# Gated, scaled and summed weights of the merge and Fourier output, prepared in the input stage and kept in DRAM

## The chip, the core and the metric

The kernel runs on one core of a Trainium2 chip. Its time is the device time of one execution in microseconds (us); the median of three runs is given. A profiled execution has a span, from its first to its last instruction, which is slightly shorter than its time.

## What is computed

One transformer block over 2048 latent tokens of width 1024, with 256 context tokens. The parts that matter here:

```python
hx = modulate(rms_norm(x, norm1_g), sh1, sc1)
fx, qx, kx, vx = split_projection(hx @ w_in)
y_four = fourier_mix(fx)                        # 4 groups of 128 channels, 2-D Fourier transform
y_attn = neighbourhood_attention(qx, kx, vx, kc, vc, rpb)
g_f, g_a = split(sigmoid(hx @ w_gate))
merged = g_f * (y_four @ w_fo) + g_a * (y_attn @ w_ao)
x = x + g1 * (merged @ w_o)
x = x + g2 * sqrelu_mlp(modulate(rms_norm(x, norm2_g), sh2, sc2), w1, w2)
```

w_fo and w_ao are 512 x 1024, w_o is 1024 x 1024, g1 is a vector of 1024 that comes from the conditioning c.

## The kernel before

Every large product is done with operands that are split in two: a rounded high half and the rest as low half, and three products (high-high, high-low, low-high) are summed by `mm3` (line 77) into one PSUM bank. So each weight must be brought to two halves before it is used: `split_on` (line 85) rounds on ScalarE (ACT) and subtracts on VectorE (DVE) or GpSimd (POOL); `halve` (line 385) does the same with a power-of-two scale.

The stages, in order:

1. **Input stage.** `run_pair` (line 767) goes through eight pairs of weight blocks in the order of `seq` (line 689): f, two gate blocks, q0 with a gate block, q1 with a gate block, v, k0 with a gate block, k1 with a gate block, and a last pair of gate blocks. Within a pair it loops over four blocks of 512 tokens (and the context tokens for k and v). Beside the matmuls run generators: `side_work` (line 294) computes the modulation vectors (g1r, the gates g1 in all 128 rows, among them), then loads all MLP weights once in 32 loads of 1 MB (w12m) to find their scales: 16 with a DVE maximum, 16 with an ACT square whose sum is accumulated. `split_values` (line 838) prepares v. When side_work ends, `early_blocks` (line 373) prepares eight blocks of MLP weights (N_EARLY), each of 1 MB, as seven scaled halves with `prepare` (line 389), and stores them in DRAM. `tick` (line 457) sets their pace: after each small unit of matmuls (a tick) it takes one step of side_work, and once that has ended, a share of a step of early_blocks (0.6 in a q or k unit, 0.8 in v, 1.5 in a gate unit). What is left of both is run out before the last pair.
2. **Last pair and `fourier_prep` (line 866).** Beside the last pair, fourier_prep folds the Fourier input and splits the tables. In its loop it also loads w_attn_out, w_out and w_fourier_out in eight loads of 1 MB (wn) and squares them on ACT, for their norms.
3. **Fourier stage.** `channel_dft`, `seq_dft`, `seq_dft64`, and `merge_scales` (line 995), which computes from the norms and the largest Fourier value the powers of two that keep the halves in range (mgs), and divides g1r by one of them.
4. **Attention.** 64 tiles of 128 queries (`order`, line 1104), two heads each, by `block` (line 1286). All loads through `fetch` (line 1048) are tied into one order on the SP queue. Beside the blocks `step` (line 1413) takes steps of `beside_attention` (line 1397): first `merge_fourier` (line 1168), which loads the rows of w_fourier_out and their mirrored rows wfr (`load_w`, line 1183), adds and subtracts them, splits the four results (ws), splits the Fourier output (ys), and does the products pmf; then `load_wa` (line 1389), which loads w_attn_out in four parts and scales, rounds and subtracts on POOL; then, from tile (3, 0, 3) plus three, `attn_out(0)` (line 1359), the merge of the first 256 tokens (products pua).
5. **Merge.** `attn_out(1)` runs while `stage_wo` (line 1522) brings w_out in eight parts through two staging buffers: DVE multiplies by g1r, ACT rounds, POOL and DVE in turn subtract (line 1536). Then for each 256 tokens: `out_proj` (line 1458, products po), `attn_out` for later tokens, and `norm_T`. PSUM has four banks for pua and po together, and the gate tiles ga, gf, ft have two buffers each.
6. **MLP.** Its weights come in halves from DRAM; the blocks that were not prepared early are prepared beside its matmuls (`prep`, line 1699) at a pace worked out from their number (`todo`, line 1783).

Within one engine, and within the SP queue, instructions run in the order in which they were queued. That order is planned when the kernel is built, from the order of the program and estimated times.

## Time and profile before

| | us |
|---|---|
| median of three runs (2656.83 to 2659.85) | 2658.93 |
| the profiled execution, time | 2660.88 |
| the profiled execution, span | 2659.1 |
| TensorE (PE) busy | 2538.6 |
| VectorE (DVE) busy | 1827.3 |
| ScalarE (ACT) busy | 1183.3 |
| GpSimd (POOL) busy | 484.4 |

A busy time is a sum over all stages, and each stage has its own limit. So the stretches of the kernel are looked at one by one (in the table of stretches, below, each engine's busy time is followed by its instructions as x and a number; PEld is TensorE's weight load): an engine that is busy for nearly the whole of a stretch sets its length, and idle time of another costs nothing there.

### The profile page before, as it was taken

The numbers are of one execution on the slowest core, as the hardware profiler recorded it, in microseconds if no ns is written. First come the engines' busy times: TensorE is split into PE (matmuls) and PEld (weight loads), VectorE is DVE, ScalarE is ACT, GpSimd is POOL, SyncE is SP. The second block draws the span as 40 slices with busy tenths as digits, with TensorE's granted clock in tenths as the row PEclk, the third lists the DMA queues.
The fourth block names the chain that finished last, engine by engine and source line by source line (L and its number), as shares of the span: only waits on it lengthen the run. The fifth ranks groups of instructions, "written<-read, shape, count | busy, mean of one in ns | idle before, by whom it ended". The sixth has DMA issues, their size and how long they took to land.

```text
span 2659.1 us, 42665 instructions
## 1 busy us (share of the span) xinstructions
PE 2538.6 (95%) x15830; PEld 1473.0 (55%) x15830; DVE 1827.3 (69%) x3672; ACT 1183.3 (44%) x2113; POOL 484.4 (18%) x715
## 2 busy tenths in 40 slices
PE   6899989898999899998999999999999999999999
PEld 5445756776656678875666444444444444444444
DVE  6756976568553678887777696978877644636367
ACT  5623225545242577874444564627351333314050
POOL 1201221012224545452000121121211100000000
PEclk9999999999999999998999999999999999999999
DMA  8577689867374744556767777787766533333334
GB/s 269 137 225 204 203 248 304 270 204 245 93 249 141 199 118 138 148 169 207 237 226 264 260 242 261 231 279 233 268 235 230 181 99 105 101 103 99 104 103 155
DMA packets 345962, 517.77 MB, mean 195 GB/s; under 512 B 48497, under 2 KB 210505, under 8 KB 341401
## 3 DMA queue, kind: packets, MB, share of 16 engines
q1 hardware_dynamic: 296425, 406.50, 48.8%
q0 software_dynamic: 29104, 75.23, 8.4%
q10 hardware_dynamic: 20224, 33.31, 3.9%
q8 instruction: 124, 2.03, 0.3%
q14 instruction: 85, 0.70, 0.1%
HBM read 370.11 MB, written 145.84 MB: 194 GB/s over the span
## 4 chain that ended last, share of the span: by engine, by line
PE 68%; DMA 11%; DVE 11%; issue 3%; ACT 3%; POOL 3%; SPq 2%; DVEq 0%; ACTq 0%; POOLq 0%
PE p L82 21%; PE pm L82 17%; PE ps_g L82 8%; PE po L82 6%; DMA w12m<-in_w_mlp 3%; PE pua L82 2%; PE ps_k L82 2%; PE tp L1325 2%; PE pmf L1263 2%; PE pv L1339 1%; SPq L188 1%; PE ps_f L82 1%; PE ps_v L82 1%; PE sc L1303 1%; DVE wo L387 1%
## 5 line engine op out<-in xcount | busy, mean ns | idle before, releaser
L82 PE MATMUL pm<-hc,wb 128*128 128x512 f16 x2688 | 582.6, 379 | 5.6 <-DVE p L1605 2.1
L82 PE MATMUL p<-wb,a 128*128 128x512 f16 x2688 | 581.9, 379 | 2.1 <-DVE X L1605 1.5
L82 PEld LDWEIGHTS <-wb 128*128 128x128 f16 x2688 | 262.9, 98 | 323.6 <-issue 7.3
L82 PEld LDWEIGHTS <-a 128*128 128x128 f16 x2688 | 263.0, 98 | 319.7 <-issue 2.9
L82 PE MATMUL ps_g<-hx,w_g 128*128 128x512 f16 x1536 | 342.5, 380 | 0.9 <-ACT ot_f L516 0.9
L1605 DVE TENSOR_TENSOR X<-X,p 128x512 f32<-128x512 f32 x280 | 184.5, 685 | 171.1 <-PE p L82 151.8
L82 PEld LDWEIGHTS <-hx 128*128 128x128 f16 x2304 | 227.4, 99 | 39.6 <-issue 7.2
L82 PEld LDWEIGHTS <-w_g 128*128 128x128 f16 x1536 | 151.0, 99 | 171.2 <-issue 3.2
L1091 POOL DMA_DIRECT2D bt<-tT x264 | 132.4, 508 | 76.3 <-DVE ri L1332 53.0
L1605 DVE TENSOR_TENSOR u<-pm,u 128x512 f32<-128x512 f32 x128 | 87.5, 690 | 84.3 <-PE pm L82 82.5
L1312 DVE CUSTOM_DVE_ANT_0 s<-sc,bt,qsc 128x736 f32<-128x736 f32 (+5 forms) x128 | 111.2, 869 | 37.1 <-PE sc L1306 33.9
L386 ACT ACTIVATE wo<-ws,msc 128x512 f16<-128x512 f32 x96 | 69.0, 718 | 152.0 <-DVE ws L430 124.0
L1609 ACT ACTIVATE p<-pm 128x512 f32<-128x512 f32 x32 | 18.9, 589 | 239.7 <-PE pm L82 239.7
L1739 POOL DMA_DIRECT2D xr<-x1d x32 | 17.3, 539 | 569.8 <-DVE X L1605 562.1
L1333 DVE SCALAR_TENSOR_TENSOR pL<-tp,pH 128x640 f16<-128x640 f32 (+1 forms) x128 | 112.3, 878 | 5.0 <-ACT pH L1328 4.5
L1316 ACT ACTIVATE s<-s,m 128x736 f32<-128x736 f32 (+5 forms) x128 | 104.6, 817 | 16.5 <-DVE m L1312 13.9
L386 ACT ACTIVATE wo<-raw,msc 128x512 f16<-128x512 f32 x128 | 87.4, 709 | 52.0 <-DVE raw L430 17.8
L82 PE MATMUL po<-wouH,mH 128*128 128x512 f16 x256 | 97.3, 384 | 9.3 <-DVE ga L1383 9.3
L1325 PE MATMUL tp<-ident,s 128*128 128x128 f32 x704 | 103.1, 281 | 0.8 <-ACT s L1316 0.7
L516 ACT ACTIVATE ot_g<-ps_g,usc_g 128x512 f32<-128x512 f32 x64 | 43.4, 681 | 130.9 <-PE ps_g L82 117.6
L82 PE MATMUL po<-wouL,mH 128*128 128x512 f16 x256 | 98.8, 386 | 2.4 <-POOL wouL L1536 2.4
L387 DVE SCALAR_TENSOR_TENSOR wo<-raw,msc,wo 128x512 f16<-128x512 f32 x128 | 94.4, 748 | 8.0 <-ACT wo L386 7.9
(535 smaller groups left out, 4645.9 us busy)
## 6 DMA issues: line engine op xcount, KB each, us to landing
wb<-w1d SPq DMA_DIRECT2D x224, 256.0 KB
wb<-w2d SPq DMA_DIRECT2D x224, 256.0 KB
w12m<-in_w_mlp SPq DMA_DIRECT2D x32, 1024.0 KB
raw<-in_w_mlp ACTq DMA_DIRECT2D x24, 1024.0 KB
w1d<-wo POOLq DMA_DIRECT2D x84, 256.0 KB, 4.0
w2d<-wo POOLq DMA_DIRECT2D x84, 256.0 KB, 4.0
gT<-ot_g SPq DMA_DIRECT2D x64, 256.0 KB
hc<-hcd SPq DMA_DIRECT2D x14, 1024.0 KB
```

The source lines that it names most:

```text
L82: last_mm[0] = pe.matmul(ps, l, r, start=(start and i == 0), stop=(stop and i == n - 1))
L188: last_load[0] = sp.dma_start(dst, src)
L386: act.activation(hi, src, AF.Copy, scale=scale)
L387: dve.scalar_tensor_tensor(out=lo, in0=src, scalar=scale, in1=hi, op0=ALU.mult, op1=ALU.subtract)
L516: act.activation(o, ps, func, scale=scale)
L1091: load_(t[i * 16:(i + 1) * 16, :, off + j0 * w:off + (j0 + 8) * w], raw(tT[ct], (2 * hp * 15 + dr) * w, [[120 * w, 16], [15 * w, 2], [1, 8 ...
L1263: pe.matmul(ps, l, r, start=(i == 0), stop=(i == len(prods) - 1))
L1312: tail["dve"] = dve.tensor_tensor_reduce(out=s[:, :n], in0=sc, in1=bias, op0=ALU.add, op1=ALU.min, scale=qsc[:, 4:5], scalar=3.0e38, accum ...
L1316: tail["act"] = act.activation(s[:, :n], s[:, :n], AF.Exp, bias=m1[:, 0:1], scale=-1.0, accum_out=m1[:, 1:2])
L1325: tail["pe"] = pe.transpose(tp[:, i * 128:(i + 1) * 128], s[:, o:o + 128], ident)
L1333: tail["dve"] = dve.scalar_tensor_tensor(out=pL[:, :c], in0=tp[:, :c], scalar=PTOP, in1=pH[:, :c], op0=ALU.mult, op1=ALU.subtract)
L1605: last["dve"] = dve.tensor_tensor(out=o, in0=x, in1=y, op=op)
```

## The change

The halves of w_attn_out (waD), of w_out times g1r (woD), and of the sums and differences of the mirrored rows of w_fourier_out (wfD) are made earlier and stored in DRAM. The eight wn loads and their squares move from fourier_prep into side_work, two to a yield, and the part of merge_scales that needs only the norms and g1r moves behind them (`branch_scales`). waD and woD are made in `branch_weights`, at the end of early_blocks. N_EARLY goes from 8 to 7, and the share of a step per q or k unit from 0.6 to 0.85. wfD is made at the end of fourier_prep. merge_fourier, load_wa and the merge then load ready halves.

```diff
@@ dit_block, side_work: after the loop over w12m
+        for j in range(8):
+            w, k = branch_rows(j)
+            wt = pb.tile([128, KT, 256], F32, tag="awt", name=f"wn{j}", bufs=2).rearrange("p k n -> p (k n)")
+            sp.dma_start(wt.rearrange("p (k n) -> p k n", k=2), w[k * 256:(k + 1) * 256, :].rearrange("(k p) n -> p k n", p=128))
+            act.activation(wt, wt, AF.Square, accum_out=wn[:, j:j + 1])
+            if j % 2:
+                yield
+        branch_scales()
...
+    def branch_scales():
+        ps = adp.tile([128, 512], F32, tag="ad", name="pwn")
+        pe.matmul(ps[:, 0:8], ones, wn, start=True, stop=True)
...
+        dve.reciprocal(mgs[:, 0:1], mgs[:, 10:11])
+        dve.reciprocal(y, mgs[:, 11:12])
+        dve.tensor_scalar(out=g1r, in0=g1r, scalar1=y, scalar2=None, op0=ALU.mult)
+
+    def branch_weights():
+        for j in range(6):
+            w, k = branch_rows(j)
+            t = pb.tile([128, KT, 256], F32, tag="awt", name=f"wb{j}", bufs=2)
...
+            sp.dma_start(t, w[k * 256:(k + 1) * 256, :].rearrange("(k p) n -> p k n", p=128))
+            yield
+            for i in range(2):
+                o = pb.tile([128, D], F32, tag="xh", name=f"wbo{j}_{i}", bufs=5).bitcast(F16).rearrange("p (o n) -> p o n", o=2)
+                if j < 2:
+                    halve(o[:, 0], o[:, 1], t[:, i], mgs[:, 0:1])
+                else:
+                    dve.tensor_tensor(out=t[:, i], in0=t[:, i], in1=g1r, op=ALU.mult)
+                    act.activation(o[:, 0], t[:, i], AF.Copy)
+                    dve.tensor_tensor(out=o[:, 1], in0=t[:, i], in1=o[:, 0], op=ALU.subtract)
+                sp.dma_start((waD, woD)[j >= 2][k][:, i * 2 * D:(i + 1) * 2 * D], o.rearrange("p o n -> p (o n)"))
+                yield
...
-    prepared, N_EARLY = set(), 8
+        yield from branch_weights()
+    prepared, N_EARLY = set(), 7
...
@@ unit_qk
-            tick(0.6)
+            tick(0.85)
...
@@ fourier_prep
-            for j in (2 * i, 2 * i + 1):
...
-                sp.dma_start(tn, w[k * 256:(k + 1) * 256, :].rearrange("(k p) n -> p k n", p=128))
-                tn = tn.rearrange("p k n -> p (k n)")
-                act.activation(tn, tn, AF.Square, accum_out=wn[:, j:j + 1])
+        fold(1)
+        yield
+        for p in range(2):
...
+                sp.dma_start(w[o:o + 64], a["w_fourier_out"][0][r0:r0 + 64, :])
+                pool.memset(wm[o:o + 1, :D], 0.0)
+                sp.dma_start(wm[o + 1:o + 64, :D], wfr[2 * p + h])
+            dve.tensor_tensor(out=t, in0=w, in1=wm[:, :D], op=ALU.add)
+            dve.tensor_tensor(out=w, in0=w, in1=wm[:, :D], op=ALU.subtract)
+            yield
+            for x, src in enumerate((t, w)):
...
+                split_on(dve, o[:, 0], o[:, 1], src)
+                for i in range(2):
+                    sp.dma_start(wfD[x, i, p], o[:, i].bitcast(F32))
                 yield
-        fold(1)
...
@@ merge_fourier
-        rows = load_w(0, fetch)
         for p in range(2):
             for x in range(2):
                 fetch(ys[x][1][:, p].bitcast(F32), yF[p][x])
+        for x in range(2):
+            for i in range(2):
+                fetch(ws[x][i].bitcast(F32), wfD[x, i].rearrange("a p n -> p a n"))
         yield
         for p in range(2):
-            w, wm, t = rows
-            dve.tensor_tensor(out=t, in0=w, in1=wm, op=ALU.add)
-            dve.tensor_tensor(out=w, in0=w, in1=wm, op=ALU.subtract)
-            yield
-            split_on(dve, ws[0][0][:, p], ws[0][1][:, p], t)
-            if p == 0:
-                rows = load_w(1, pool.dma_start)
-            yield
-            split_on(dve, ws[1][0][:, p], ws[1][1][:, p], w)
-            yield
...
@@ beside_attention
-        wa = [pm.tile([128, 4, D], F16, tag="wa" + o, name="wa" + o) for o in "HL"]
-        load_wa()
+        wa = pm.tile([128, 2, 2, 2, D], F16, tag="wa", name="wa")
+        for k in range(2):
+            fetch(wa[:, k].rearrange("p k o n -> p (k o n)"), waD[k])
...
@@ merge
     attn = attn_out(1, mmp, pg)
-    for k in range(8):
+    for k in range(4):
         next(attn)
-        wt = stage_wo(k)
-        dve.tensor_tensor(out=wt, in0=wt, in1=g1r, op=ALU.mult)
-        act.activation(wo[0][:, k, :], wt, AF.Copy)
-        (pool, dve)[k % 2].tensor_tensor(out=wo[1][:, k, :], in0=wt, in1=wo[0][:, k, :], op=ALU.subtract)
+        sp.dma_start(wo[:, k].rearrange("p k o n -> p (k o n)"), woD[k])
```

## Rows read from the trace of the kernel before

**Rows 1.** Page, part 1: busy us, share of the span, instructions.

```profile
PE 2538.6 (95%) x15830; PEld 1473.0 (55%) x15830; DVE 1827.3 (69%) x3672; ACT 1183.3 (44%) x2113; POOL 484.4 (18%) x715
```

**Rows 2.** Stretches: us, busy PE PEld DVE ACT POOL, clock, DMA share, GB/s.

```profile
240.00:340.00 100.00, 100.00 (x705) 70.24 (x703) 91.24 (x299) 34.18 (x76) 23.47 (x21) 1.00 0.76 220
374.00:455.00 81.00, 69.70 (x472) 46.68 (x473) 60.40 (x155) 36.09 (x67) 14.25 (x13) 0.96 0.92 300
455.00:500.00 45.00, 37.37 (x319) 31.54 (x317) 12.05 (x43) 23.73 (x39) 1.11 (x2) 0.96 0.79 261
600.00:640.00 40.00, 31.65 (x240) 23.22 (x238) 31.65 (x79) 17.50 (x37) 9.67 (x8) 0.98 0.85 270
660.00:760.00 100.00, 100.00 (x701) 68.96 (x700) 56.95 (x173) 34.30 (x66) 22.04 (x22) 1.00 0.41 125
760.00:840.00 80.00, 80.00 (x387) 38.14 (x385) 24.84 (x37) 31.28 (x47) 19.95 (x16) 1.00 0.64 220
889.80:912.00 22.20, 14.64 (x150) 11.24 (x150) 18.86 (x57) 15.54 (x31) 14.55 (x25) 0.92 0.86 229
890.00:942.00 52.00, 35.05 (x419) 27.51 (x417) 48.42 (x110) 40.35 (x80) 24.66 (x43) 0.93 0.67 166
1180.00:1214.30 34.30, 29.55 (x365) 25.51 (x364) 28.97 (x67) 22.48 (x52) 7.50 (x5) 0.95 0.46 141
1225.00:1234.00 9.00, 0.18 (x2) 0.11 (x2) 8.90 (x12) 2.53 (x3) 1.22 (x1) 0.71 0.91 320
1249.00:1261.30 12.30, 12.22 (x49) 5.19 (x49) 3.44 (x5) 2.21 (x3) 2.64 (x3) 0.86 0.73 235
1580.00:2000.00 420.00, 418.49 (x1939) 189.60 (x1938) 344.76 (x540) 209.33 (x337) 81.67 (x151) 1.00 0.76 253
```

**Rows 3.** On w_out's tiles: ns min/median/max, first and last start.

```profile
L1534 DVE TENSOR_TENSOR wou<-wou,g1r x8: 1212/1217/1224, 1192.4 to 1242.4; 128x1024 f32<-128x1024 f32 x8
L1535 ACT ACTIVATE wouH<-wou x8: 1041/1057/1058, 1220.7 to 1243.6; 128x1024 f16<-128x1024 f32 x8
L1536 POOL TENSOR_TENSOR wouL<-wou,wouH x4: 2115/2217/9937, 1221.8 to 1249.0; 128x1024 f16<-128x1024 f32 x4
```

**Rows 4.** PE's waits, whole span: us in total, times, longest.

```profile
PE po L82 <- DVE ga L1383: 9.3, 2, 8.8
PE ps_v L82 <- ACT vo_v L646: 6.5, 4, 3.7
PE po L82 <- POOL wouL L1536: 2.4, 1, 2.4
PE pua L82 <- POOL yaL L1366: 1.9, 1, 1.9
PE sc L1303 <- DMA Q<-qH: 1.9, 1, 1.9
```

**Rows 5.** Chain that ended last, PE pieces: start us, us, what.

```profile
512.79 2.63 PE ps_v L82 x24
1314.83 13.17 PE po L82 x61
1328.00 10.48 PE pua L82 x96
```

**Rows 6.** DVE groups, 890 to 942: count, busy us, mean ns, idle.

```profile
L1207 DVE TENSOR_TENSOR ws<-wf,wm 128x1024 f32<-128x1024 f32 x2 | 2.4, 1218 | 0.0
```

**Rows 7.** Timeline: last Q load of row block 1, its first matmul.

```profile
904.58 2.92 SPq L1051 DMA_DIRECT2D Ql<-qL  x2
912.00 0.31 PE L1303 MATMUL sc<-k,Q 128*128 128x360 f16 x1 [0.90 <-DVE m L1312]
```

**Rows 8.** Timeline: two ACT squares; and the early MLP blocks' halves on DVE.

```profile
455.97 1.91 ACT L340 ACTIVATE w12m<-w12m 128x2048 f32<-128x2048 f32 x1
486.83 1.91 ACT L340 ACTIVATE w12m<-w12m 128x2048 f32<-128x2048 f32 x1 [1.24 <-DMA w12m<-in_w_mlp]
L387 DVE SCALAR_TENSOR_TENSOR wo<-raw,msc,wo x32: 742/746/752, 499.3 to 669.6; 128x512 f16<-128x512 f32 x32
```

More of the change, by code (lines that the diff above doesn't have):

```diff
@@ L113, in dit_block @@
     wfr = scratch("wfr", [4, 63, D])
+    waD = scratch("waD", [2, 128, 4 * D], F16)
+    woD = scratch("woD", [4, 128, 4 * D], F16)
+    wfD = scratch("wfD", [2, 2, 2, 128, D])
     mF = scratch("mF", [8, 128, S])
@@ L1006, in merge_scales @@
         pe.matmul(ps[:, 0:1], ones[0:1, :], mgs[0:1, 6:7], start=True, stop=True)
-        pe.matmul(ps[:, 8:16], ones, wn, start=True, stop=True)
         dve.tensor_copy(y, ps[:, 0:1])
         ws = mgs[:, 7:10]
-        for i, (j, n) in enumerate(((0, 2), (2, 4), (6, 2))):
-            dve.tensor_reduce(out=ws[:, i:i + 1], in_=ps[:, 8 + j:8 + j + n], axis=AX.X, op=ALU.add)
-        pool.tensor_tensor(ws, ws, half[:, 0:3], op=ALU.pow)
         dve.scalar_tensor_tensor(out=b, in0=ws[:, 0:1], scalar=PTOP * VTOP * 512 ** 0.5, in1=vsc[:, 2:3], op0=ALU.mult, op1=ALU.mult)
@@ L1181, in merge_fourier @@
         ys = [pairs("ya"), pairs("yb")]
-        def load_w(p, fetch):
-            w, wm, t = (stage(f"w{o}{p}") for o in "fms")
-            for h in range(2):
-                o, r0 = 64 * h, (2 * p + h) * 128
-                fetch(w[o:o + 64], wf[r0:r0 + 64, :])
-                pool.memset(wm[o:o + 1], 0.0)
-                fetch(wm[o + 1:o + 64], wfr[2 * p + h])
-            return w, wm, t
         s64 = []
@@ L1203, in merge_fourier @@
                 fetch(ys[x][1][:, p].bitcast(F32), yF[p][x])
+        for x in range(2):
+            for i in range(2):
+                fetch(ws[x][i].bitcast(F32), wfD[x, i].rearrange("a p n -> p a n"))
         yield
         for p in range(2):
-            w, wm, t = rows
-            dve.tensor_tensor(out=t, in0=w, in1=wm, op=ALU.add)
-            dve.tensor_tensor(out=w, in0=w, in1=wm, op=ALU.subtract)
-            yield
-            split_on(dve, ws[0][0][:, p], ws[0][1][:, p], t)
-            if p == 0:
-                rows = load_w(1, pool.dma_start)
-            yield
-            split_on(dve, ws[1][0][:, p], ws[1][1][:, p], w)
-            yield
             for x in range(2):
@@ L1379, in attn_out @@
             for k in range(4):
-                mm3(ps, [(wa[0][:, k, ms], wa[1][:, k, ms], yH[:, k, :], yL[:, k, :])], k == 0, k == 3)
+                w = wa[:, k // 2, k % 2]
+                mm3(ps, [(w[:, 0, ms], w[:, 1, ms], yH[:, k, :], yL[:, k, :])], k == 0, k == 3)
                 if k == 1 and t == 0:
@@ L1387, in attn_out @@
             yield
-    def load_wa():
-        for k in range(4):
-            wt = pm.tile([128, D], F32, tag="wst", name=f"wao{k}", bufs=2)
-            fetch(wt, a["w_attn_out"][0, k * 128:(k + 1) * 128, :])
-            pool.tensor_scalar(wt, wt, mgs[:, 0:1], None, op0=ALU.mult)
-            pool.tensor_copy(wa[0][:, k, :], wt)
-            pool.tensor_tensor(wa[1][:, k, :], wt, wa[0][:, k, :], op=ALU.subtract)
     def beside_attention():
@@ L1448, in dit_block @@
     pg = sbuf("mgb", "right")
-    wo = [pg.tile([128, 8, D], F16, tag="wo" + o, name="wou" + o) for o in "HL"]
+    wo = pg.tile([128, 4, 2, 2, D], F16, tag="wo", name="wou")
     normed, x1s, x1r = {}, [], iter(range(0, S, 128))
@@ L1467, in out_proj @@
             ps = mmp.tile([128, 512], F32, tag="mm", name=f"po{nm}_{n}")
-            mm3(ps, [(mH[:, k, cs], mL[:, k, cs], wo[0][:, k, ns], wo[1][:, k, ns]) for k in range(KT)])
+            mm3(ps, [(mH[:, k, cs], mL[:, k, cs], *(wo[:, k // 2, k % 2, o, ns] for o in range(2))) for k in range(KT)])
             dve.scalar_tensor_tensor(out=x1[:, ns], in0=ps, scalar=mgs[:, 3:4], in1=x1[:, ns], op0=ALU.mult, op1=ALU.add)
```

36 lines of the change are left out of this document (19 added, 17 removed).

## The prediction, made before the changed kernel was run

> **What bounds the kernel now.** I read the busy totals first, then a table of stretches, then TensorE's (PE's) waits, and last single lines. PE is busy for 95% of the span [rows 1], so only what PE loses can be won, and what the added work makes it lose must be paid. The table of stretches [rows 2] shows where it loses. From 240 to 340, 660 to 760 and 760 to 840 us PE is busy the whole time: work beside it is free there. In 455 to 500 it loses 45 - 37.37 = 7.6 us, in 600 to 640 it loses 8.35. In 890 to 942, where attention starts, it is busy for 35.05 of 52 while VectorE (DVE) is busy for 48.42: DVE is the bound. From 1214.3 to 1261.3 (the entry to the merge) PE does 96 pua and 96 po matmuls; it is idle for nearly the whole of 1225 to 1234 and runs at a mean granted clock of 0.86 in 1249 to 1261.3. In the MLP (1580 to 2000) it loses 1.5 of 420. The profiled execution has a span of 2659.1 and a time of 2660.9; the median of the runs is 2658.9, 0.07% under it. The sum below is made on the profile and taken off the median.
>
> **What the change removes.**
> *Entry to the merge.* Eight loads of 512 KB through two staging buffers, eight DVE multiplications by g1r (1.217 each), eight ScalarE (ACT) roundings (1.057) and eight subtractions, four on DVE and four on GpSimd (POOL), the longest of these 9.94 us [rows 3]. PE waits 8.8 us for DVE and 2.4 for that POOL subtraction [rows 4]. At full speed 61 po matmuls take 13.17 us and 96 pua 10.48 [rows 5], 0.216 and 0.109 each, so 47 us hold 96 x 0.216 + 96 x 0.109 = 31.2 us of work: 15.8 are lost, of which 11.2 are waits and the rest is slow clock after them. DVE loses 8 x 1.22 + 4 x 1.22 = 14.6 us of work. What comes late next is data: the same 4 MB (now ready-made) cannot start before attention lets go of its buffers at about 1214, and 1225 to 1234 already moves 320 GB/s [rows 2]. 4.2e6 bytes at 320 are 13.1 us, so the last part lands at about 1227.5 and the gate tiles that queue behind it some 2 us later. PE stops at about 1225, so some 4.6 us of idling and 2 us of slow clock stay: gain 9. Bounds: 2.4 (only the POOL wait goes) to 15.8.
> *End of attention.* The POOL work of load_wa and its four 512 KB loads with their waits go; two 1 MB loads take their place. PE's 1.9 us for Q, queued behind those loads, and 1.9 for yaL go [rows 4], with some of the 34.3 - 29.55 = 4.75 us lost in 1180 to 1214.3 [rows 2]. I take 5; bounds 0 and 6.7.
> *Start of attention.* DVE loses eight passes of 1.218 us [rows 6] (two additions, two subtractions, four low halves) and two over the same 1,024 columns for g1r, in all ten, 12 us of the 48.42 [rows 2]. ACT loses four roundings. Against it stands a queue. SP loads 1 MB of rows and 2 MB of yF ahead of the Q of the next row block; now it loads 2 MB and 4 MB. That is 3 MB more, and at the 229 GB/s of 889.8 to 912 [rows 2] that takes 13.7 us. The last Q load was issued at 904.6 to 907.5 and its first matmul ran at 912.0 [rows 7], after a DVE wait: Q was in time by 4 us at most. So Q becomes late by some 10 us, while DVE uses the gap for the four splits of yF (four passes of the same length) that it now does after 912. 12 minus 10 plus part of those 4.9 leaves 3. Bounds: -9 (the splits don't move up) to +12 (Q lands in time).
> *Last pair and merge_scales.* Eight ACT squares (1.91 us for one of this shape [rows 8]) and their 8 MB leave the last pair; DVE gets 8 x 1.22 us, and 6 MB are loaded or stored. DVE is busy for 24.84 of 80 us there, PE for 80.00: nothing either way. If the tail slid past 840, it would delay the Fourier stage by up to 5.
>
> **What it adds.**
> *The v pair.* The eight 1 MB loads with their squares now run in side_work, two to a yield, after the 32 loads of the MLP weights. Eight of the 16 squares of w2 run from 455.97 to 486.83, 4.41 us apart, in a stretch where PE loses 7.6 us [rows 2, 8], since behind a square that waits for its load stand ACT's vo evictions, which free PSUM (6.5 us of PE's waits are on them [rows 4]) and whose stores queue on SP with the loads. That is 0.95 us of PE per load: eight more cost 7.6, take 8. Lower bound 0: from 240 to 340 loads at 220 GB/s cost PE nothing. Upper bound: if PE goes no faster than the squares, 8 x 4.41 = 35.3 us pass while the four ticks hold 4 x 2.63 = 10.5 us of PE work [rows 5]: 24.8. I take the near row, the same pair and queue. The matmul on wn and the chain of branch_scales wait for the last square; they are in the 8.
> *The k pairs.* branch_weights puts on DVE eight multiplications and eight subtractions of 1.22 and four low halves of about as much, 24.5 us; on ACT 12 x 1.06 = 12.7; and 12 MB on SP. One MLP block leaves (seven halves of 0.746 [rows 8] and four sums of about that on DVE, 8 us). Side_work ends four ticks later, and with 0.85 for 0.6 per tick the 68 steps just fit before the last pair. Its cover is 660 to 760, where DVE is idle for 43 us, ACT for 66, and the DMA share is 0.41. Cost 1; bounds 0 and 8, what 600 to 640 loses with a like mix.
> *The MLP.* One more block to prepare, 8 us of DVE beside 75 idle ones in 1580 to 2000: 1; bounds 0 and 2.
>
> Sum: -9 - 5 - 3 + 8 + 1 + 1 = -7, so 2658.9 - 7 = **2652**.
>
> **The rivals.**
> *The added loads are hidden* (chance 0.22). If the squares are queued where the loads have landed, the v pair costs 0 and the rest 2: -17 + 2 = -15, 2644. For it: 240 to 340. Against: the 7.6 us beside the same kind of load.
> *The merge is bound by its transfers* (0.15). po starts no earlier, since the gate tiles land behind 4 MB; only the POOL wait goes (2.4), attention's start gives nothing, its end 5: -7.4 + 10 = +2.6, 2661.5. For it: the DMA share of 0.91 in 1225 to 1234. Against: DVE busy for 8.90 of those 9 us.
> *Q waits for the weights* (0.10). Attention stalls at row block 1 by more than DVE gains, -9 in place of +3: -9 - 5 + 9 + 10 = +5, 2664. It decides if the Q loads land after about 920. The Trainium skill, "DMA: Bandwidth & Descriptors", section "Issuing engines are not separate DMA queues", speaks for this side: transfers from all issuing engines share the same 16 DMA engines, so the smaller load on the POOL queue would buy the SP queue no separate path. By the 358 GB/s of "SBUF — State Buffer", section "Summary: rules for kernel authors", the 3 MB would take an estimated 8.8 us and the start of attention would give about 7 in place of 3; no stretch above shows that rate.
> *The v pair runs at the pace of the loads* (0.17), the case on the slower side: -17 + 24.8 + 2 = +9.8, 2668.7. Its place is ACT's queue from about 487 us; it decides where two loads hold a tick for more than about 6 us. For it: 300 GB/s at a DMA share of 0.92 in 374 to 455, so twice the loads per tick can't all flow. Against: the v pair has 36 ticks, and nothing but queue order ties four of them to these loads.
>
> **The numbers.** My forecast has 0.36, from 2645 to 2658. About 0.2%, 5.3 us, is what a measurement of this kernel can tell from no change: faster means below 2653.6, slower above 2664.2. Faster: 0.27 of the forecast and all of the first rival, 0.49. Slower: most of the v pair's 0.17, half of the Q case and a little of the transfers, 0.22. The rest, 0.29, is no change. The range reaches from 2637 (loads hidden, merge and attention near their upper bounds) to 2669 (the v pair at its worst).
>
> **What would show it.** PE's 8.8 and 2.4 us before po, and its 1.9 us for Q and yaL: gone or cut to about 4.6 in all at the merge. In 890 to 942: DVE less full, and a PE wait on a Q load near 912 of at most 10 us. In the v pair: ps_v waits on vo of about 14 us in place of 6.5; over 25 would be the slower rival, none the hidden one. 660 to 840 should stay at full PE. The prediction is wrong as to mechanism if the time between 500 and 760 grows by more than 8 us, or if the merge keeps an idle stretch of 8 us with DVE no longer full.

## The result: slower by 0.4%, and the profile after

The changed kernel takes 2673.32 us (median of 6 runs, 2670.23 to 2677.69), the kernel before 2662.89 beside it (six runs, the three of the median 2658.93 among them): the ratio is 1.0041, with a 95% interval of 1.0026 to 1.0055. The forecast was 2652, with a range up to 2669 and a chance of 0.22 for slower. The profiled execution has a span of 2674.1 us, against 2659.1 before, so 15.0 us are to be found. The medians lie 10.4 apart, so some 4.6 of the 15.0 belong to these two executions and not to the change.

The work falls into stages whose bounds are the first and the last matmul on a tile (ps_v for the v pair, ps_k for the k pairs, pc for the Fourier stage, sc and pv for attention, po for the merge). First the changed kernel, by stretches with those bounds: v pair, k pairs, last pair, Fourier stage, attention, attention's end to the first po, merge, MLP. The columns are those of [rows 2].

```profile
448.50:565.60 117.10, 102.56 (x882) 88.11 (x881) 48.00 (x130) 71.75 (x107) 3.11 (x5) 0.96 0.84 280
565.60:767.50 201.90, 187.84 (x1302) 130.07 (x1300) 153.60 (x386) 87.51 (x159) 46.12 (x39) 0.97 0.70 232
767.50:856.30 88.80, 88.80 (x417) 40.83 (x416) 41.21 (x60) 24.78 (x41) 22.88 (x19) 1.00 0.56 193
856.30:909.40 53.10, 50.61 (x266) 41.30 (x265) 26.70 (x69) 11.17 (x31) 36.80 (x59) 0.87 0.67 179
909.40:1231.30 321.90, 300.51 (x3723) 248.02 (x3723) 263.89 (x591) 252.00 (x566) 131.25 (x255) 0.97 0.54 160
1231.30:1253.80 22.50, 10.65 (x100) 9.43 (x97) 8.30 (x17) 3.52 (x7) 0.00 (x0) 0.81 0.76 279
1253.80:1497.60 243.80, 243.66 (x1457) 144.60 (x1457) 165.81 (x331) 99.20 (x176) 10.16 (x15) 0.99 0.66 228
1497.60:2674.10 1176.50, 1163.70 (x5392) 527.51 (x5390) 803.97 (x1257) 451.77 (x728) 124.98 (x231) 1.00 0.57 186
```

The same stages of the kernel before:

```profile
448.80:556.10 107.30, 98.79 (x880) 86.47 (x879) 53.14 (x127) 60.98 (x96) 3.18 (x5) 0.98 0.82 272
556.10:748.20 192.10, 183.43 (x1302) 128.91 (x1300) 133.02 (x364) 76.04 (x146) 41.29 (x38) 0.98 0.53 169
748.20:837.00 88.80, 88.80 (x417) 40.87 (x416) 29.54 (x52) 35.71 (x53) 18.19 (x15) 1.00 0.65 215
837.00:889.90 52.90, 50.53 (x266) 41.49 (x265) 26.75 (x69) 11.17 (x31) 36.86 (x59) 0.87 0.63 171
889.90:1214.50 324.60, 299.99 (x3725) 246.79 (x3725) 275.30 (x613) 256.30 (x570) 162.18 (x276) 0.98 0.53 150
1214.50:1233.90 19.40, 10.58 (x98) 9.25 (x96) 16.39 (x22) 6.47 (x10) 4.39 (x2) 0.87 0.80 275
1233.90:1482.20 248.30, 245.49 (x1457) 145.05 (x1458) 174.20 (x338) 104.63 (x181) 22.18 (x17) 0.98 0.68 233
1482.20:2659.10 1176.90, 1163.79 (x5393) 527.51 (x5390) 797.25 (x1246) 448.09 (x721) 121.21 (x224) 1.00 0.56 183
```

The first column after the bounds is the length. The v pair is longer by 9.8 us and the k pairs by 9.8; the last pair, with PE busy in all of it, the Fourier stage and the MLP stand within 0.4. Attention gains 2.7, the way to the first po loses 3.1, the merge itself gains 4.5. So the input stage pays 19.6 and everything behind it gives back 4.1.

**Attention** hides two movements. Its first 96 score matmuls (three row blocks of the first heads) take 65.5 us in place of 72.4, so the start gives 6.9; from there to the end it takes 256.5 in place of 252.2, which loses 4.3. The stretch from the first score on, after and before:

```profile
909.40:931.00 21.60, 14.43 (x150) 10.88 (x150) 16.71 (x42) 16.41 (x33) 9.93 (x18) 0.92 0.90 308
...
909.40:961.40 52.00, 42.84 (x481) 32.76 (x481) 40.04 (x92) 40.30 (x86) 20.82 (x41) 0.93 0.64 199
```

```profile
889.90:911.50 21.60, 14.54 (x150) 11.20 (x150) 18.36 (x54) 15.09 (x30) 14.06 (x24) 0.92 0.86 226
...
889.90:941.90 52.00, 35.05 (x419) 27.49 (x419) 48.32 (x109) 40.35 (x80) 24.66 (x43) 0.94 0.67 166
```

DVE falls from 48.32 to 40.04 of 52 us and PE rises from 35.05 to 42.84. The first 21.6 us, with the 3 MB more, cost PE nothing (14.43 after, 14.54 before): they moved at 308 GB/s, where 226 had been reached before. At the end of attention the waits of PE, after and before:

```profile
PE pua L82 <- ACT yaH L1401: 2.2, 1, 2.2
PE pua L82 <- POOL yaL L1402: 2.0, 1, 2.0
PE pv L1375 <- DMA vt<-v: 1.7, 1, 1.7
PE sc L1339 <- DMA Ql<-qL: 1.5, 1, 1.5
...
PE sc L1339 <- DMA Q<-qH: 0.7, 1, 0.7
```

```profile
PE pua L82 <- POOL yaL L1366: 1.9, 1, 1.9
PE sc L1303 <- DMA Q<-qH: 1.9, 1, 1.9
PE pua L82 <- ACT yaH L1365: 0.8, 1, 0.8
```

The wait for yaL is still there, so it was not the work of load_wa: in the kernel before GpSimd had stood idle for 7.2 us ahead of that subtraction of 2.1 us; now a product (ft) that waited for its load stands just ahead of it. The waits for loads are 3.9 in place of 1.9: two loads of 1 MB stand ahead of Q and vt as four of 512 KB did. The size of this loss is uncertain: where the queues have the same order up to there, the stretch behind the first 96 score matmuls takes 252.4 to 256.8 us (after, e2, e5, e6 and e9 in the table below). The gain that was forecast is in none of them.

**The entry to the merge.** PE's wait for the gate (ga) grew from 8.8 [rows 4] to 11.8 us, and the wait for the GpSimd subtraction is gone (it came behind the first po, so its 2.4 us are part of what the merge gains). PE's waits from 1225 to 1262:

```profile
PE po L82 <- DVE ga L1420: 11.8, 1, 11.8
```

What SP's queue waited for from 1200 to 1260 (L1411 are the gate tiles, L1555 the weights), and the issues on its timeline:

```profile
SPq L1411 <- DVE ga L1421: 24.0, 6, 13.9
...
SPq L1555 <- DMA yA<-yo: 1.2, 1, 1.2
```

```profile
1220.27 0.92 SPq L1411 DMA_DIRECT2D gf<-gT  x1
1235.14 0.36 SPq L1411 DMA_DIRECT2D ft<-mF  x1
1237.14 1.99 SPq L1555 DMA_DIRECT2D wou<-woD  x4
1239.23 0.38 SPq L1411 DMA_DIRECT2D ft<-mF  x1
1239.66 0.50 SPq L1411 DMA_DIRECT2D ga<-gT  x1
```

SP issues nothing between 1221.2 and 1235.14, where a gate tile waits for its buffer (13.9 us); the weight loads come behind it, wait 1.2 us more for attention's last store (yA), start at 1237.14, and the gate tiles of the next rows (ft, ga at 1239) stand behind their 4 MB. The stretch that these take:

```profile
1237.10:1252.40 15.30, 4.83 (x45) 4.18 (x43) 3.76 (x8) 1.47 (x2) 0.00 (x0) 0.76 0.93 347
```

At its end the gate tiles have landed and DVE goes on; PE was busy for 4.83 of its 15.3 us.

**The input stage.** In the v pair PE's waits for vo rise from 6.5 [rows 4] to 12.7: 10.0 in the row below, and 2.7 in rows with the tiles of the context tokens (ps_v0c, ps_v1c, vo_v1c). Another 1.8 are for the last square (wn).

```profile
PE ps_v L82 <- ACT vo_v L698: 10.0, 6, 3.1
```

In the k pairs PE loses time in two places where it lost little before, the first 34 us and the stretch in which the branch weights are made; after, then before:

```profile
565.60:600.00 34.40, 30.59 (x204) 20.68 (x202) 18.28 (x51) 12.56 (x25) 5.25 (x6) 0.90 0.54 174
...
674.00:730.00 56.00, 52.17 (x373) 36.39 (x371) 50.42 (x111) 26.59 (x43) 17.64 (x12) 1.00 0.89 315
```

```profile
556.10:590.00 33.90, 33.58 (x237) 22.84 (x235) 20.09 (x54) 14.97 (x28) 5.96 (x6) 1.00 0.55 171
...
660.00:710.00 50.00, 50.00 (x363) 35.57 (x362) 28.67 (x88) 16.72 (x34) 12.95 (x13) 1.00 0.42 139
```

In 565.6 to 600 PE loses 3.8 us and has a mean granted clock of 0.90 (from 572.7 on it is at the lower of its two levels, 1.2 GHz, for 6.8 us); before, in the same place, it lost 0.3 at full clock. In 674 to 730 DVE is busy for 50.42 of 56 and PE loses 3.8; before, in 660 to 710, DVE had 21 us free and PE lost nothing. The first loss is a wait of 3.8 us for the value scale (vsc), which needs the last eviction of v. PE's wait, and ACT's in the same stretch:

```profile
PE pvm L894 <- DVE vsc L892: 3.8, 1, 3.8
```

```profile
ACT vo_v L698 <- DMA vF<-vo_v: 5.8, 1, 5.8
```

ACT makes that eviction 5.8 us late, because the buffer that it writes is still being stored (vF).

What this first loss is worth is less than it looks. Of the 1,224 matmuls on the tiles of k and of its gate blocks, the changed kernel needs 20.4 us for the first 96 and 100.7 for the first 576 (before: 14.0 and 96.7). e5, below, has the same order there, waits 1.4 us for vsc in place of 3.8 and keeps the full clock:

```profile
567.80:602.20 34.40, 32.99 (x231) 22.35 (x230) 20.10 (x56) 13.77 (x26) 5.89 (x6) 1.00 0.54 177
```

It needs 15.1 us for the first 96, but 102.0 for 576: its later waits are longer (5.6 us for usc_k, the scale of the next weight block, where the changed kernel waits 1.9). So of the k pairs' loss 4.0 us arise up to there, whether the wait for vsc is long or short, and 5.7 behind (101.3 us in place of 95.6).

### The profile page after: what moved, and what is told of

The parts are those of the page before. It is cut to its first block, busy times and chain, and to the rows that moved or that the text cites. A ratio compares the mean times of both kernels' runs of the same rounds, so it can differ in the third digit from the quotient of the medians.

```text
span 2674.1 us, 42746 instructions
## 1 busy us (share of the span) xinstructions
PE 2547.4 (95%) x15830; PEld 1478.2 (55%) x15830; DVE 1832.2 (69%) x3681; ACT 1184.8 (44%) x2117; POOL 452.9 (17%) x702
## 4 chain that ended last, share of the span: by engine, by line
PE 64%; DVE 12%; DMA 11%; ACT 3%; issue 3%; POOL 1%; SPq 1%; ACTq 0%; DVEq 0%; POOLq 0%
PE p L82 21%; PE pm L82 17%; PE ps_g L82 7%; PE po L82 6%; DMA w12m<-in_w_mlp 3%; PE pua L82 3%; PE tp L1361 2%; PE pmf L1299 2%; PE pv L1375 2%; PE sc L1339 1%; DVE wo L439 1%; DMA raw<-in_w_mlp 1%; DVE a L1624 1%; PE ps_k L82 1%; PE sc L1342 1%
## 5 line engine op out<-in xcount | busy, mean ns | idle before, releaser
L82 PEld LDWEIGHTS <-w_g 128*128 128x128 f16 x1536 | 151.9, 100 | 177.5 <-issue 11.8
L82 PE MATMUL po<-wou,mH 128*128 128x512 f16 x512 | 154.3, 383 | 12.0 <-DVE ga L1420 11.8
L1369 DVE SCALAR_TENSOR_TENSOR pL<-tp,pH 128x640 f16<-128x640 f32 (+1 forms) x128 | 112.3, 878 | 8.5 <-ACT pH L1364 7.9
L438 ACT ACTIVATE wo<-raw,msc 128x512 f16<-128x512 f32 x128 | 88.0, 710 | 45.2 <-DMA raw<-in_w_mlp 16.5
L82 PE MATMUL ps_v<-w_v,hx 128*128 128x256 f16 x768 | 90.3, 280 | 10.9 <-ACT vo_v L698 10.0
## 6 DMA issues: line engine op xcount, KB each, us to landing
wb<-w1d SPq DMA_DIRECT2D x224, 256.0 KB
wb<-w2d SPq DMA_DIRECT2D x224, 256.0 KB
w2d<-wo POOLq DMA_DIRECT2D x91, 256.0 KB, 3.9
w1d<-wo POOLq DMA_DIRECT2D x84, 256.0 KB, 3.9
gT<-ot_g SPq DMA_DIRECT2D x64, 256.0 KB
```

What stands on the lines that cost most here:

```text
L82: last_mm[0] = pe.matmul(ps, l, r, start=(start and i == 0), stop=(stop and i == n - 1))
L438: act.activation(hi, src, AF.Copy, scale=scale)
L1369: tail["dve"] = dve.scalar_tensor_tensor(out=pL[:, :c], in0=tp[:, :c], scalar=PTOP, in1=pH[:, :c], op0=ALU.mult, op1=ALU.subtract)
```

## The experiments

The table has all kernels: the median, the ratio to the kernel before measured beside it with its interval (it is made from the single runs and is not the quotient of two medians), and the stages of the profiled execution (v pair, k pairs, last pair and Fourier stage, first 96 scores, rest of attention, from there to the first po, merge, MLP). A stage differs from run to run: the v pair takes 112.3 to 119.3 us in after, e2, e5, e6 and e9, in which ACT, DVE and SP work in the same order up to its end, and 102.0 to 107.3 in before, e3 and e7; the k pairs 200.5 to 201.8 in the first group without e2, and 192.1 to 193.3 in the second.

| kernel | us | ratio | v | k | last+F | 96 | rest | to po | merge | MLP |
|---|---|---|---|---|---|---|---|---|---|---|
| before | 2662.9 | | 107.3 | 192.1 | 141.7 | 72.4 | 252.2 | 19.4 | 248.4 | 1172.4 |
| after | 2673.3 | 1.0041 [1.0026, 1.0055] | 117.1 | 201.8 | 141.9 | 65.5 | 256.5 | 22.4 | 243.8 | 1172.1 |
| e1 | 2673.8 | 1.0034 [1.0019, 1.005] | 115.6 | 194.1 | 143.6 | 71.8 | 249.7 | 20.5 | 250.4 | 1172.9 |
| e2 | 2667.3 | 1.0021 [1.0007, 1.0034] | 116.2 | 197.5 | 140.3 | 65.9 | 256.8 | 22.5 | 243.5 | 1171.4 |
| e3 | 2681.8 | 1.0068 [1.0049, 1.0087] | 105.9 | 193.3 | 148.8 | 66.6 | 269.9 | 17.8 | 248.4 | 1172.4 |
| e5 | 2674.7 | 1.0043 [1.0028, 1.0058] | 119.3 | 201.2 | 143.5 | 66.6 | 252.4 | 25.0 | 244.6 | 1172.8 |
| e6 | 2664.2 | 1.0019 [1.0006, 1.0031] | 112.3 | 200.5 | 141.3 | 66.0 | 253.6 | 16.8 | 244.4 | 1171.2 |
| e7 | 2665.3 | 1.001 [0.9999, 1.0022] | 102.0 | 192.1 | 141.6 | 72.4 | 252.1 | 20.0 | 247.8 | 1172.4 |
| e8 | 2663.9 | 1.0013 [0.9999, 1.0026] | 113.2 | 194.9 | 142.7 | 64.9 | 255.2 | 22.3 | 243.7 | 1171.3 |
| e9 | 2668.9 | 1.0032 [1.002, 1.0043] | 113.8 | 200.5 | 143.1 | 65.2 | 256.8 | 21.0 | 243.9 | 1171.3 |
| e10 | 2661.0 | 0.9989 [0.9978, 1.0001] | 109.2 | 197.1 | 145.9 | 65.2 | 256.0 | 17.5 | 243.3 | 1171.4 |
| e11 | 2659.1 | 0.9987 [0.9975, 0.9999] | 110.8 | 193.1 | 140.5 | 65.0 | 263.8 | 10.4 | 243.1 | 1177.8 |
| e12 | 2663.5 | 1.0006 [0.9991, 1.0021] | 103.4 | 208.3 | 141.5 | 66.2 | 256.6 | 17.1 | 243.0 | 1171.5 |
| e13 | 2660.6 | 0.9992 [0.9978, 1.0006] | 100.7 | 195.1 | 141.9 | 69.9 | 253.0 | 19.5 | 247.1 | 1172.6 |

**e1: the squares alone, in the kernel before.** The loop of the change in side_work, with branch_scales behind it, and no weights made:

```diff
+        for j in range(8):
+            w, k = branch_rows(j)
...
+            act.activation(wt, wt, AF.Square, accum_out=wn[:, j:j + 1])
+            if j % 2:
+                yield
+        branch_scales()
```

> The kernel before with one part of the change: the eight 1 MB loads with their squares, and the scales made of them, run in the v pair; no weights are made beforehand and nothing else is moved. Theory A (the squares wait for their loads on ACT's queue and hold up the evictions of the v pair): the v pair goes from 107.3 to about 117 us, the k pairs stay within 3 us of 192.3, the last pair stays at 88.8: about +10 us on the kernel before. Rival B (what the changed kernel lost in the k pairs is also a consequence of side_work ending four ticks later): the k pairs lose 5 to 10 us here too, +15 to +20 in all. Rival C (the squares are hidden, and the v pair's loss came with what was queued after it): within 3 us of the kernel before.

Measured: 1.0034 [1.0019, 1.005]; the v pair 8.3 us longer, the k pairs 2.0, the last pair 88.8 as before. Theory A holds. That the squares left the last pair gained nothing there; that they entered the v pair cost 8 us, and 10.7 by the means of the two groups above. Most of the k pairs' loss is not here, so rival B falls: the rest comes with what else the change puts there, the branch weights and the faster pace of 0.85 per tick.

**e2: no arithmetic on the branch weights.**

```diff
-                if j < 2:
-                    halve(o[:, 0], o[:, 1], t[:, i], mgs[:, 0:1])
-                else:
-                    dve.tensor_tensor(out=t[:, i], in0=t[:, i], in1=g1r, op=ALU.mult)
-                    act.activation(o[:, 0], t[:, i], AF.Copy)
-                    dve.tensor_tensor(out=o[:, 1], in0=t[:, i], in1=o[:, 0], op=ALU.subtract)
+                pool.memset(o, 0.0)
```

> The changed kernel in which the twelve halves of the scaled weights are not computed: the six 1 MB loads and twelve 512 KB stores stay, and each half that is stored is filled with zeros by GpSimd in place of the DVE and ACT arithmetic, so attention's projection and the merge work on zero weights. Theory A (the k pairs are slowed by DVE's queue: 24.5 us of added DVE work): the k pairs go from 202.0 back to about 193 to 195 us, so 7 to 9 us faster than the changed kernel; the rest as in the changed kernel. Rival B (12 MB more on the SP queue and on the DMA engines slow the k pairs): they stay at 200 to 203 us, the time within 3 us of the changed kernel.

Measured: the k pairs take 197.5 in place of 201.8, between the two theories. The stretch in which the loads and stores of the weights run:

```profile
671.00:715.00 44.00, 43.19 (x305) 29.86 (x304) 29.77 (x84) 12.67 (x26) 32.24 (x24) 1.00 1.01 375
```

It moves 375 GB/s, and PE loses 0.8 of 44 us. So the loads and stores do not slow PE there, and most of the 3.8 us of 674 to 730 is DVE's arithmetic. Up to 679 us the order on ACT, DVE, GpSimd and SP is that of the changed kernel, and the first part of the loss stays: 101.0 us for the first 576 matmuls (1.9 us of waits for vsc). The other 648 take 96.6, in place of 101.3 in the changed kernel and of 99.4 to 100.3 in e5, e6 and e9: the arithmetic costs 3 to 5 us.

**e3: the Fourier weights alone, in the kernel before.** fourier_prep makes and stores them, merge_fourier loads them:

```diff
+            for x, src in enumerate((t, w)):
...
+                split_on(dve, o[:, 0], o[:, 1], src)
+                for i in range(2):
+                    sp.dma_start(wfD[x, i, p], o[:, i].bitcast(F32))
...
-        rows = load_w(0, fetch)
+        for x in range(2):
+            for i in range(2):
+                fetch(ws[x][i].bitcast(F32), wfD[x, i].rearrange("a p n -> p a n"))
```

> The kernel before with the third part of the change alone: the Fourier weights are added, subtracted and split in the last pair and kept in DRAM, and the start of attention loads them; the squares stay in the last pair as well. Theory A (the 7 us that the changed kernel is ahead after 96 score matmuls of attention come from this part, and the last pair hides it): the last pair stays within 1 us of 88.8, the first 96 score matmuls take 65 to 67 us in place of 72.3, and 5 to 7 us remain at the end: 0.2 to 0.3% faster than before. Rival B (the lead is given back at the end of attention, where Q and the weights of its projection queue, as in the changed kernel): lead of 7 us at 96 score matmuls, 0 to 2 us at the first po matmul. Rival C (with the squares also there, the last pair overflows): the last pair takes 3 to 8 us longer and the time is the same or slower.

Measured: 1.0068, slower than the whole change. The first 96 scores do take 66.6 us, so the gain at the start is this part's. But the Fourier stage takes 7.1 us longer, since DVE comes 6.3 late to it, and the rest of attention 17.7. PE's waits from 843 us, and SP's queue from 1120 to 1185:

```profile
PE sc L1307 <- DMA Q<-qH: 18.9, 2, 17.3
PE pc L960 <- DVE gL L90: 6.3, 1, 6.3
```

```profile
SPq L1072 <- POOL waL L1399: 23.5, 2, 21.9
```

The work beside attention reaches load_wa earlier; two of its loads wait in SP's queue up to 21.9 us for staging buffers that GpSimd has still to empty, Q stands behind them, and PE waits 17.3 us for one Q. Rivals B and C are right in kind: the lead is given back, and by more than B had, and the overflow shows in the Fourier stage, not in the last pair (88.8). It shows by how much an early load in a shared queue can cost, and what the ready-made waD is good for: with it no load of the projection waits for GpSimd.

**e5: the merge weights in four tiles, on GpSimd's queue.**

```diff
-    wo = pg.tile([128, 4, 2, 2, D], F16, tag="wo", name="wou")
+    wo = [pg.tile([128, 2, 2, D], F16, tag=f"wo{k}", name=f"wou{k}") for k in range(4)]
...
-        sp.dma_start(wo[:, k].rearrange("p k o n -> p (k o n)"), woD[k])
+        pool.dma_start(wo[k].rearrange("p k o n -> p (k o n)"), woD[k])
```

> The changed kernel with the merge weights in four tiles of 1 MB in place of one, loaded through the GpSimd queue in place of the SP queue. Theory A (the one tile lies over all the memory of attention and its loads stand in SP's queue behind a gate tile that waits, so none starts before 1237 and the gate tiles of the second chunk land behind 4 MB): at least one load starts before attention ends, the others 4 to 8 us earlier than 1237, and PE's wait of 11.8 us before po falls to 3 to 7: 4 to 8 us faster than the changed kernel. Rival B (the entry to the merge is bound by 4 MB at the DMA rate after attention, whatever the queue): the loads start within 2 us of the same time and the wait stays at 10 to 12 us: within 2 us of the changed kernel.

Measured: nothing gained, rival B by its numbers: the loads start at 1237.77, PE waits 14.4. But in the compiled kernel's memory map (which no trace shows) the first of the four tiles, and it alone, lies over the tile from which attention stores its last output (yo); the three others, over the bias tables, queue behind it on GpSimd. That is a third theory: not the rate and not the queue, but the memory under the first load.

**e6: the residual tiles allocated first.** As e5, and

```diff
     pg = sbuf("mgb", "right")
+    x1t = [pg.tile([128, D], F32, tag="x1", name=f"x1_{r}", bufs=3) for r in (0, 128)]
```

so that x1 lies over yo and the weights over the bias tables.

> The changed kernel with the four weight tiles on the GpSimd queue as in the run before, and with the residual tiles (x1) allocated ahead of them, so that the first weight tile no longer lies over the output tile that attention's last store reads. Theory A (what holds the loads is the memory under them: in the changed kernel, and with four tiles too, the first one waits for that last store): wou0 and wou1 start before attention ends, wou2 and wou3 within 2 us of its end, PE's wait before po falls from 11.8 to 0 to 4 us, the stretch from attention's end to the first po from 22.4 to 11 to 15: 7 to 11 us faster than the changed kernel. Rival B (the gate tiles wait behind 4 MB in the DMA engines, wherever they start): the loads start early, but the wait stays above 8 us: 0 to 3 us faster.

Measured: 1.0019 in place of 1.0041, and from attention's end to the first po 16.8 in place of 22.4 us. The four loads on GpSimd's timeline, and PE's wait:

```profile
1199.05 0.61 POOL L1556 DMA_DIRECT2D wou<-woD  x1 [5.09 <-DVE ri L1368]
1199.85 0.57 POOL L1556 DMA_DIRECT2D wou<-woD  x1 [0.19 <-issue]
1217.79 0.54 POOL L1556 DMA_DIRECT2D wou<-woD  x1 [17.37 <-DVE ri L1368]
1221.53 0.54 POOL L1556 DMA_DIRECT2D wou<-woD  x1 [3.21 <-PE pv L1375]
```

```profile
PE po L82 <- DVE ga L1420: 6.2, 1, 6.2
```

Attention ends at 1221.4 in this run: three loads start ahead of that, the last with it. The wait for attention's last store (yA<-yo) has moved to the load of the residual rows, 1.9 us on SP, as the new layout has it. PE's wait falls to 6.2, above the 0 to 4 that were expected; 1.5 MB of residual rows still stand ahead of the next gate tiles, but no run tests whether that is the reason. The intervals of the two ratios touch (1.0031 and 1.0026); the gain is read from the stage and its wait.

**e9: that allocation alone** (one weight tile, SP's queue; the edit is the added line of e6).

> The changed kernel with that allocation order alone: one weight tile, SP queue. Theory A: the loads wait for attention's last PE work in place of its last store, and still stand in SP's queue behind a gate tile that waits until about 1235: they start 2 us earlier than 1237.1 at most, PE's wait stays at 9 to 12 us: 0 to 3 us faster than the changed kernel. Rival B (the memory is all that holds them, not the queue): they start at 1231 to 1233, the wait falls to 5 to 8 us: 4 to 6 us faster.

Measured: the loads start at 1234.91, PE waits 10.4: theory A. With the memory free, the queue still holds them (1.4 us gained to the first po); e5 and e9 each took one of two locks away, e6 both.

**e7: the same allocation in the kernel before** (the same added line).

> The kernel before with the same allocation order, nothing else changed. Theory A (before, too, the scaled weights are written into memory that attention's last store holds, and DVE's multiplications pile up behind it): the stretch from attention's end to the first po falls from 19.4 to 13 to 16 us, the wait for the GpSimd subtraction goes: 4 to 8 us faster than the kernel before. Rival B (DVE's work or the two staging buffers are the bound there): within 2 us of the kernel before.

Measured: 20.0 us to the first po, waits of 9.4 and 2.6: rival B. There the loads go through staging buffers, seven of them at 1215.9 to 1236.5, and the layout is not what binds them.

**e8: squares over 128 of 2,048 columns** (an estimate of the norms).

```diff
-            act.activation(wt, wt, AF.Square, accum_out=wn[:, j:j + 1])
+            act.activation(wt[:, :128], wt[:, :128], AF.Square, scale=4.0, accum_out=wn[:, j:j + 1])
```

> The changed kernel with the eight squares taken over the first 128 of 2,048 columns (times 4 before squaring, so that the sum is an estimate of the whole): ACT's work for them falls from 15 us to about 2, the loads and the waits for them stay. Theory A (a square costs the v pair because it waits for its load ahead of the evictions): the v pair stays at 113 to 117 us. Rival B (ACT's own work in the squares is the cost): it falls to 108 to 111 us, 6 to 9 us faster than the changed kernel.

Measured: the v pair takes 113.2, inside the spread of the kernels with whole squares: theory A. Unexpected were the k pairs, 194.9 in place of 200.5 to 201.8: PE's wait for vsc at their start is 0.7, at full clock. PE's waits from 560 to 768, and the first stretch:

```profile
PE pvm L894 <- DVE vsc L892: 0.7, 1, 0.7
```

```profile
562.10:600.00 37.90, 37.22 (x270) 26.16 (x268) 25.39 (x68) 17.03 (x33) 6.51 (x8) 1.00 0.64 209
```

In this kernel the order differs from 552 us on: SP stores v's last values ahead of an early block's halves, and ACT evicts them ahead of the next pair's weights. So the loss at the start of the k pairs goes with how v's last evictions and stores stand in the queues; whether ACT's 13 us or the order is what counts, this run does not tell.

**e10: the eight squares on DVE**, on top of e6:

```diff
-            act.activation(wt, wt, AF.Square, accum_out=wn[:, j:j + 1])
+            dve.tensor_tensor(out=wt, in0=wt, in1=wt, op=ALU.mult)
+            dve.tensor_reduce(out=wn[:, j:j + 1], in_=wt, axis=AX.X, op=ALU.add)
```

> The kernel with the early merge loads (the run before, e6) in which the eight squares of the branch weights are made on DVE (a multiplication and a sum, some 4.5 us each, where DVE was idle for 69 of the v pair's 117 us) in place of ACT (15 us). Theory A (the squares cost because they stand in ACT's queue ahead of the evictions of v, and the last of these come late into the first k pair, where PE waits 3.2 to 3.8 us and then runs at half clock): the v pair falls from 112 to 117 us to 107 to 110, the k pairs from 200.5 to 194 to 196, PE's wait for the value scale to under 1.5: 8 to 12 us faster than e6, so faster than the kernel before. Rival B (the loads bound the v pair, 8 MB more at the DMA rate, on whatever engine the squares stand): the v pair stays at 112 to 117 and the k pairs within 2 us of 200.5: no change. Rival C (DVE's queue is blocked in ACT's place): slower than e6 by 3 us or more.

Measured: the v pair 109.2, the k pairs 197.1, no wait for the value scale: theory A in kind. The matmuls on v's tiles from the 289th to the 576th, beside which the squares run, take 32.9 us, in place of 44.2 in the changed kernel and 33.9 before. The k pairs gain less than expected, because DVE's work is pushed back into them: it is busy for 167.6 us there, against 153.6 in the changed kernel. Against e6, 1.0019, it is at 0.9989 [0.9978, 1.0001].

**e11: five early blocks in place of seven, three gate buffers in place of two**, on top of e10:

```diff
-    prepared, N_EARLY = set(), 7
+    prepared, N_EARLY = set(), 5
...
-    name=f"{n_}{t}_{m}", bufs=2) for n_ in ("ga", "gf", "ft"))
+    name=f"{n_}{t}_{m}", bufs=3) for n_ in ("ga", "gf", "ft"))
```

> As e10, with two things in stages apart from each other: five MLP blocks prepared early in place of seven, and three buffers in place of two for the gate tiles of the merge. Theory A (in the k pairs DVE is the bound while the branch weights are made, 50.4 busy of 56 us from 674 to 730 in the changed kernel, and PE loses 3.8 there): with two blocks less the k pairs lose 3 to 6 us against e10, and the MLP pays 0 to 1 for them. Rival B (the loads and stores of the branch weights are the bound there): the k pairs stay within 2 us of e10. For the merge: if the gate tiles' buffers hold the second half of the chunk's gates, the stretch from attention's end to the first po falls from 16.8 to 11 to 14 us; if the DMA engines do (1.5 MB of residual rows ahead of them), it stays within 1.5 us of 16.8.

Measured: the k pairs 193.1, as theory A has it, but the MLP pays 6.4 for the two blocks, not 0 to 1. The first po comes 7.1 us sooner after attention and attention takes 7.8 longer: the gate work has only moved ahead of attention's end. In all 0.9987 [0.9975, 0.9999]: 0.1% under the kernel before, and not to be told from e10 and e13.

**e12 and e13: the last eight squares of w_mlp2 on DVE too**, on top of e10 and in the kernel before:

```diff
-                act.activation(wt, wt, AF.Square, accum_out=w2m[:, j:j + 1])
+                if i < 24:
+                    act.activation(wt, wt, AF.Square, accum_out=w2m[:, j:j + 1])
+                else:
+                    dve.tensor_tensor(out=wt, in0=wt, in1=wt, op=ALU.mult)
+                    dve.tensor_reduce(out=w2m[:, j:j + 1], in_=wt, axis=AX.X, op=ALU.add)
```

> As e10 (early merge loads, the squares of the branch weights on DVE), with the last eight squares of the MLP's second weights on DVE too, so that no square stands in ACT's queue in the v pair. Theory A (squares that wait for a 1 MB load ahead of the evictions of v are what the v pair loses, in the kernel before as well): the v pair falls from 109.2 to 101 to 105 us, PE's waits for vo from 5.0 to under 1.5; 3 to 8 us faster than e10, 0.2 to 0.4% faster than the kernel before. Rival B (the loads themselves bound it): within 2 us of 109.

> The kernel before with those eight squares of the MLP's second weights on DVE and nothing of the change. Theory A: the v pair falls from 107.3 to 101 to 103 us, PE's waits for vo from 6.5 to under 1.5, 4 to 6 us faster than the kernel before. Rival B (the loads bound it): within 2 us of 107. Rival C (DVE's evictions and value maxima queue behind the loads in ACT's place): PE's waits move to DVE, and the time is the same or slower.

Measured: the v pair falls to 103.4 and 100.7, PE's waits for vo to 0.6 and 0.2 (e12, then e13). For the waits that is theory A, with nothing taken from the loads. The stage gains less. Counted up to the first matmul of k it takes 106.9 and 102.3, since in e12 scales are still being made between the two pairs; and e7, which up to there is the kernel before, had 102.0 with waits of 4.1. No gain in time is shown, 1.0006 [0.9991, 1.0021] and 0.9992 [0.9978, 1.0006]: in e12 the k pairs take 208.3, DVE is busy for 178.1 of them, and nearly all of PE's waits there are for DVE; in e13 they take 195.1, with 2.3 us for vsc and 1.6 for vo at their start. PE's waits in the v pair and two stretches of the k pairs of e12, and PE's waits in the v pair of e13:

```profile
PE ps_v L82 <- ACT vo_v L703: 0.6, 1, 0.6
```

```profile
556.00:600.00 44.00, 39.44 (x257) 26.70 (x257) 38.81 (x108) 28.02 (x45) 10.02 (x9) 0.92 0.70 237
600.00:650.00 50.00, 43.41 (x302) 31.06 (x303) 42.10 (x111) 24.65 (x48) 11.92 (x9) 0.95 0.90 286
```

```profile
PE ps_v L82 <- ACT vo_v L650: 0.2, 1, 0.2
```

## Why the prediction was wrong, by its own steps

The sum was -7; the profile shows +15, the medians +10.4. Both signs that the prediction named against its mechanism came: the time between 500 and 760 grew by more than 8 us (the two stages there by 19.6), and the merge kept an idle stretch of 11.8 us with DVE busy for 3.76 of 15.3. Term by term:

- *Entry to the merge, -9: +3.1 to the first po and -4.5 behind it, so -1.4.* The step that failed is "cannot start before attention lets go of its buffers at about 1214", with the last part landed 13 us later. Loads into the place of the weights wait for attention's last store and for a gate tile in SP's queue; they started 5.8 us after attention's end (1231.3), not at it, and the gate tiles landed 15 us after that. The rival "the merge is bound by its transfers" named what was seen, gate tiles that land behind 4 MB, but e6 shows that this is no bound of the rate: with the same 4 MB started from 22 us ahead of attention's end up to that end, 5.6 us came back. The wait for GpSimd went, as forecast.
- *End of attention, -5: +4.3.* The step that failed is that PE's waits for Q and yaL "go". The wait for yaL was put down to load_wa; GpSimd was idle ahead of that subtraction before, and the wait is 2.0 after. Q waits behind two 1 MB loads as it did behind four smaller ones. Of the 4.3, 2.0 are such waits for loads and 1.4 the wait for yaH; kernels alike up to there lie between 252.4 and 256.8, before, e1, e7 and e13 between 249.7 and 253.0, so the loss is known to some us only.
- *Start of attention, -3: -6.9.* Right in its cause (DVE's passes), too small because of the 10 us by which Q was to be late: 3 MB more were priced at 229 GB/s and ran at 308, and PE's waits for Q and Ql there were 1.1 us. With Q in time the prediction's own bound was 12; it stayed at 6.9, with PE busy for 28.4 of the 30.4 us from 931 on, so DVE was no longer what bound it there. The rival with Q late past 920 did not happen.
- *Last pair, Fourier stage and MLP, 0, 0 and +1: 0.0, 0.2 and -0.4.* The cover that was named held. e11 shows its limit: two blocks more, and the MLP pays 6.4.
- *v pair, +8: +9.8* (e1: +8.3). Place and cause were right, and the size nearly: the near row, 0.95 us per load, was the better of the two bounds. The size is known to some us only, as the stage itself differs by 7 between like executions; the two groups are 10.7 apart by their means. PE's waits for vo were 12.7, with 1.8 for the last square, where about 14 stood; the mean clock of the pair fell from 0.98 to 0.96 besides.
- *k pairs, +1, upper bound 8: +9.8.* The step that failed is "its cover is 660 to 760, where DVE is idle for 43 us". The added DVE work comes in one stretch, 674 to 730, and fills DVE to 90% there: 3.8 us, of which e2 takes 3.0 away. And side_work ending four ticks later was counted as a shift that costs nothing: the first 576 matmuls of the k pairs take 4.0 us longer, and 3.7 to 5.3 in e2, e5, e6 and e9. In the changed kernel the place of this loss is the first 34 us (3.8 us of waiting and some 3.4 of clock), in e5 it is further on. The late end of side_work alone is not all of it: e1, which has it at the old pace of 0.6, needs 97.8 (before 96.7). In e8 and e10, with the squares shortened or out of ACT's queue and the pace at 0.85, the loss is gone (94.8 and 91.1); in e10 DVE's work is then paid behind it. No run separates the order of the queues, the squares and the pace further.

The sign was lost by the entry to the merge (7.6 us off), the end of attention (9.3) and the k pairs (8.8). In hindsight the chance for slower should have been larger: the gains least in doubt were DVE's at the start of attention, and most others hung on a load starting on time in a queue shared with the work it was to speed up. The Trainium skill, "DMA: Bandwidth & Descriptors", section "Issuing engines are not separate DMA queues", says that DMAs from all issuing engines run on the same 16 DMA engines. e5 agrees with it: with the weights on GpSimd's queue and the gate tiles on SP's, the gate tiles came no sooner (PE's wait was 14.4 us, in the changed kernel 11.8). e6 and e9 show what queue and memory decide beside that, when a load starts. What remains open: what binds the first 576 matmuls of the k pairs, the 6.2 us before po that stay in e6, and the 7 us by which the v pair differs between runs with one and the same order of its queues.

## What to carry to other kernels

Work moved to where an engine has time on average can still fill it in the stretch where it lands: compare its length with the idle time of that stretch alone, and count what the moved work delays behind it. A load that replaces arithmetic is worth only what its start allows: look at what tile lies under its target and what waits ahead of it in its queue; here both had to be cleared before more than 1.4 us was gained. And an accumulation that waits for a load is better kept out of the queue of the engine that frees PSUM, if the engine that takes it has the time: on DVE the eight squares of the change cost less (e10 beside e6, 0.9989 and 1.0019), eight more gained nothing that could be told from noise (e12, e13).
